# The order of every engine's queue, computed inside the kernel by list scheduling, for a two-layer retention and stick-breaking trunk

## The chip, the cores and the metric

The kernel runs on one core of one Trainium2 chip. The metric is device time in microseconds of one execution of the whole program. A core has five instruction queues that run side by side: TensorE (PE; its weight loads are listed apart as PEld), VectorE (DVE), ScalarE (ACT), GpSimd (POOL) and SyncE (SP), which here issues all the DMA transfers. Each queue is executed in its own order, which is fixed when the program is built. An instruction that waits for another engine or for a transfer holds back everything behind it in its queue.

## The reference

Two layers over a residual stream of 1024 tokens by 1024 features, in float32. Layer 0 is a retention with four heads, layer 1 a stick-breaking attention with eight heads whose keys and values come from one shared projection of the stream between the layers.

```python
u = rms_norm(h, ret_norm_pre[i])
q, k, v, g = jnp.split(u @ ret_w_in[i], ...)
q, k = rope(q, pos), rope(k, pos) * RET_QK_DIM ** -0.5
o = retention_chunkwise(q, k, v)              # o_t = sum_{s<=t} gamma_h^(t-s) (q_t . k_s) v_s
o = (o - mu) * lax.rsqrt(var + EPS)
y = (merge_heads(o) * jax.nn.silu(g)) @ ret_w_out[i]
h = h + rms_norm(y, ret_norm_post[i])
k_shared, v_shared = jnp.split(rms_norm(h, kv_norm) @ w_kv, [SB_QK_WIDTH], axis=-1)
...
q, g = jnp.split(rms_norm(h, sb_norm_pre[j]) @ sb_w_in[j], [SB_QK_WIDTH], axis=-1)
z = q @ k^T / sqrt(128)
weights = where(s < t, sigmoid(z_ts) * prod_{s<j<t} (1 - sigmoid(z_tj)), 0)
y = (merge_heads(weights @ v) * jax.nn.silu(g)) @ sb_w_out[j]
h = h + rms_norm(y, sb_norm_post[j])
```

## The kernel before

The stream is held transposed, features on the 128 partitions, and worked in two halves of 512 tokens. `run` (L1200) goes through four phases: retention for the first and the second half ("A", 0 and 1), then attention for the first and the second half ("C", 0 and 1). A phase has four turns, one for a retention head or for a pair of attention heads.

Every product is made of three float32r matmuls, `mm3` (L122 to L127): each operand is split into a rounded part and the rest, and high x high, high x low and low x high are summed in a PSUM bank. So nearly everything that enters a matmul passes first through `split` (L284 to L291): ACT writes the rounded part (L287, or L290 with a gain), then DVE writes the rest (L288, or L291). Weights come in 256 KB loads into the ring `wraw` of 6 buffers, in some phases also into `ko`, `S` and `vo` (`rings`, L1193), and are split into `whl`, which has 3 buffers of 1024 columns each.

Some projections are done with fewer products from sums and differences of blocks of weights and of activations: `vg` (L480) for retention, where DVE makes the weight sums (L507, L510, L513, L516), and `values` (L859) for attention, whose sums for later use are written to DRAM by `w_sums` (L799, sums L813 to L816).

Around the matmuls stand: the evacuation of banks (ACT copies L225, L531; DVE sums L227, L535, L946; gates L458, L459, L1001, L1002 and L1088); the rotary step `rope` (L425), which goes DVE, POOL (L431, L432), and then through a split; the norms, whose sums of squares are added on POOL (L256, L412, L730); the residual steps, in which loaded tiles are scaled and added on DVE or POOL (L720, L721, L1116, L1117); the transposes of gated outputs (L693) and of attention weights (L1064) on PE, followed by a split into `oT` or `AT`; and the stick-breaking product, `rows` (L1009): two sigmoids on ACT (L1027, L1028), two masks on POOL (L1032, L1033), a scan (L1034) and a product (L1035) on DVE. `finish` (L1122) does the last output projection, norm, and store.

PSUM has eight banks, two for each of the tags `ma`, `mb`, `z` and `o`. SBUF tiles have tags too; `BUFS` (L42) gives the buffers of each.

What sets the order: the program is written as lists of small steps that `merge` (L234) and `weave` (L147) interleave, so that side work (scores, gates, norms, the next weights through `ahead`, L157) is traced between the matmuls of a main projection. From the traced program the framework's own scheduler makes each engine's queue: it walks a simulated machine with its own table of times, and of the instructions that are ready there it issues the one that stands first in the program. It hands out a tag's buffers in that walk. The kernel sets no order edges of its own; the name `keep` (L80) is defined and never used.

## Time and profile before

| | |
|---|---|
| median of 3 runs | 1777.57 us (1775.73 to 1785.08) |
| the profiled execution, span from first to last instruction | 1776.7 us |
| mean granted TensorE clock | 0.993 |
| PE busy | 1717.6 us (97%), 8036 matmuls |
| PEld busy | 1417.6 us (80%) |
| DVE busy | 1295.9 us (73%), 2131 instructions |
| ACT busy | 871.0 us (49%), 1630 instructions |
| POOL busy | 282.9 us (16%), 377 instructions |
| DMA | 348.79 MB, 59.0% of 16 engines' span |

A group row of the profile names line, engine, operation, output tile <- input tiles and shape, then the count, busy time and mean time of one, and after the second bar the idle time of the engine just before these instructions, with what ended it. A timeline row has the start and the duration in us, and in brackets the engine's idle time before the instruction and what ended that. The view of waits lists who waited for whom: us in total, how often, the longest.

### The profile page before, as it was taken

What the parts mean: (1) busy time and instruction counts of PE and PEld (TensorE: products, weight loads), DVE (VectorE), ACT (ScalarE), POOL (GpSimd) and SP (SyncE); (2) the same over time, 40 slices, a digit from 0 to 9 for tenths busy, and PEclk for the clock granted to TensorE, in tenths of its full rate; (3) what the DMA queues carried; (4) which work ended last, traced back from release to release, by engine and by line L of the source; (5) the groups of instructions that cost most, each with busy time, mean ns of one, the idle gap of its engine ahead of it and who ended that gap; (6) DMA issues with size and microseconds to landing.
All of it is one profiled execution on the core that took longest, in us unless ns stands there. A gap on an engine that the chain in (4) does not pass through costs nothing.

```text
span 1776.7 us, 24193 instructions
## 1 busy us (share of the span) xinstructions
PE 1717.6 (97%) x8036; PEld 1417.6 (80%) x8036; DVE 1295.9 (73%) x2131; ACT 871.0 (49%) x1630; POOL 282.9 (16%) x377
## 2 busy tenths in 40 slices
PE   8999999999999899999999999999999999999997
PEld 7888788778788687878877888888887788888776
DVE  8757767898866968687788767668777656756765
ACT  6435545454444535355545435545564444545541
POOL 0210412332304320101112000000210010000003
PEclk9999999999999999999999999999999999999999
DMA  5226475658546756376886988568783763552513
GB/s 192 84 101 196 153 237 173 202 184 276 165 134 199 234 162 219 94 260 201 294 304 213 321 298 270 185 207 279 253 277 109 240 207 104 161 202 95 183 66 119
DMA packets 182380, 348.79 MB, mean 196 GB/s; under 512 B 20336, under 2 KB 24560, under 8 KB 182256
## 3 DMA queue, kind: packets, MB, share of 16 engines
q1 hardware_dynamic: 182256, 347.26, 59.0%
q8 instruction: 63, 1.03, 0.2%
q14 instruction: 61, 0.50, 0.1%
HBM read 273.78 MB, written 73.40 MB: 195 GB/s over the span
## 4 chain that ended last, share of the span: by engine, by line
issue 26%; PE 14%; DVE 10%; DMA 3%; POOL 2%; ACT 1%; SPq 0%; POOLq 0%; DVEq 0%; ACTq 0%
PE pmb L127 2%; PE pmb L125 2%; PE pmb L126 2%; PE pma L125 2%; PE pma L127 2%; PE pma L126 2%; DVE sgn L1034 2%; DVE whl L288 1%; DVE whl L291 1%; POOL sgn L1032 1%; DMA S<-y 1%; DVE A L1035 1%; PE po L126 1%; PE po L127 1%; PE po L125 1%
## 5 line engine op out<-in xcount | busy, mean ns | idle before, releaser
L288 DVE TENSOR_TENSOR whl<-wraw,whl 128x512 fp32r<-128x512 f32 x323 | 229.3, 737 | 50.3 <-ACT whl L287 50.0
L287 ACT ACTIVATE whl<-wraw 128x512 fp32r<-128x512 f32 x323 | 190.7, 624 | 100.0 <-PE pmb L127 42.9
L125 PE MATMUL pmb<-xh,whl 128*128 128x512 f32 x384 | 153.6, 400 | 1.6 <-DVE sg L1002 1.5
L125 PE MATMUL pma<-xh,whl 128*128 128x512 f32 x384 | 153.8, 400 | 0.0
L127 PE MATMUL pmb<-xh,whl 128*128 128x512 f32 x384 | 150.7, 393 | 0.0
L127 PE MATMUL pma<-xh,whl 128*128 128x512 f32 x384 | 150.7, 392 | 0.0
L126 PE MATMUL pma<-xh,whl 128*128 128x512 f32 x384 | 150.3, 391 | 0.0
L126 PE MATMUL pmb<-xh,whl 128*128 128x512 f32 x384 | 150.2, 391 | 0.0
L1032 POOL TENSOR_SCALAR_AFFINE_SELECT sgn<-sgn 128x128 f32<-128x128 f32 x64 | 28.3, 442 | 684.7 <-ACT sgn L1027 623.6
L1034 DVE TENSOR_TENSOR_SCAN sgn<-sgn 128x128 f32<-128x128 f32 (+3 forms) x64 | 89.0, 1390 | 26.8 <-POOL sgn L1032 26.8
L287 ACT ACTIVATE AT<-pz 128x512 fp32r<-128x512 f32 (+1 forms) x96 | 46.5, 486 | 119.7 <-PE pz L1064 119.7
L290 ACT ACTIVATE whl<-wraw,gn 128x256 fp32r<-128x256 f32 (+1 forms) x144 | 81.0, 602 | 48.4 <-PE pmb L127 30.5
L291 DVE SCALAR_TENSOR_TENSOR whl<-wraw,gn,whl 128x256 fp32r<-128x256 f32 (+1 forms) x144 | 83.4, 611 | 21.7 <-ACT whl L290 19.1
L125 PE MATMUL pmb<-oT,whl 128*128 128x512 f32 x240 | 95.7, 399 | 3.0 <-DVE sg L1002 3.0
L287 ACT ACTIVATE whl<-S 128x512 fp32r<-128x512 f32 x104 | 64.1, 629 | 66.8 <-DVE S L510 17.2
L127 PE MATMUL pmb<-oT,whl 128*128 128x512 f32 x240 | 94.6, 394 | 1.1 <-DVE whl L288 1.1
L126 PE MATMUL pmb<-oT,whl 128*128 128x512 f32 x240 | 94.1, 392 | 0.0
L288 DVE TENSOR_TENSOR AT<-pz,AT 128x512 fp32r<-128x512 f32 (+1 forms) x96 | 52.8, 552 | 54.0 <-ACT AT L287 53.8
L125 PEld LDWEIGHTS pmb<-xh,whl 128*128 128x128 f32 x384 | 72.5, 189 | 17.4 <-DVE sg L1002 3.7
L127 PEld LDWEIGHTS pmb<-xh,whl 128*128 128x128 f32 x384 | 72.4, 188 | 16.0
L127 PEld LDWEIGHTS pma<-xh,whl 128*128 128x128 f32 x384 | 72.4, 189 | 15.7
L126 PEld LDWEIGHTS pmb<-xh,whl 128*128 128x128 f32 x384 | 72.5, 189 | 13.5
(384 smaller groups left out, 4708.5 us busy)
## 6 DMA issues: line engine op xcount, KB each, us to landing
wraw<-in_wts_dram SPq DMA_DIRECT2D x522, 256.0 KB, 3.6
y<-f SPq DMA_DIRECT2D x120, 256.0 KB, 3.4
f<-y SPq DMA_DIRECT2D x88, 256.0 KB, 3.6
S<-in_wts_dram SPq DMA_DIRECT2D x44, 256.0 KB, 4.0
vo<-in_wts_dram SPq DMA_DIRECT2D x42, 256.0 KB, 4.7
ko<-in_wts_dram SPq DMA_DIRECT2D x40, 256.0 KB, 4.6
T<-AT SPq DMA_DIRECT2D x32, 256.0 KB, 3.6
sc<-T SPq DMA_DIRECT2D x16, 512.0 KB, 4.9
```

Source lines behind the costliest of these rows:

```text
L125: MM(p, lh, rh, start=start, stop=False, **kw)
L126: MM(p, lh, rl, start=False, stop=False, **kw)
L127: MM(p, ll, rh, start=False, stop=stop, **kw)
L287: A_.activation(dst[0], src, AF.Copy)
L288: V.tensor_tensor(dst[1], src, f32(dst[0]), ALU.subtract)
L290: A_.activation(dst[0], src, AF.Copy, scale=scale)
L291: V.scalar_tensor_tensor(dst[1], src, scale, f32(dst[0]), ALU.mult, ALU.subtract)
L1032: G.affine_select(n[:, dg], n[:, dg], [[-1, 128]], ALU.is_gt, 1.0, base=0, channel_multiplier=1)
L1034: V.tensor_tensor_scan(n[:, :W][:, ::-1], n[:, :W][:, ::-1], n[:, :W][:, ::-1], 1.0, ALU.mult, ALU.bypass)
L1035: V.tensor_tensor(a[:, :W - 1], a[:, :W - 1], n[:, 1:W], ALU.mult)
```

## The change

After the whole program is traced, `arrange` reads the instruction list of the block. For each instruction on the five engines it finds which tiles it reads and writes, at a grain of 32 elements, and from this the instructions that it must follow (`before`, and the mirror `after`); `behind` and `next` are the same for two reads on one engine. `_time` gives each a time that it holds its engine and a time until its result is there; `HAND` is the time of a hand-over to another engine.

`latest` counts latest starts backward: from the matmuls in the order of the program, through the read/write graph, and through the reuse of buffers (the last uses of a tile come before the first use of the tile that takes its buffer). `place` then runs the five engines forward in these times: when an engine is free, it takes of the instructions that are ready the one with the earliest latest start. A tag's tiles are opened in program order, each when one of the tag's buffers is free. DMA transfers share one ring; a two-input DVE operation that overlaps a long POOL addition is charged 400 ns more. Last, each engine's list is written out as order edges between neighbours, of a kind that fixes the order and needs no semaphore.

The diff, cut: `_size` and `_cells` (which count elements, and mark the touched 32-element cells of a tile) and some bookkeeping are left out.

```diff
+HAND = {"PE": 100.0, "DVE": 60.0, "Activation": 60.0, "Pool": 100.0, "SP": 50.0}
...
+def _time(s, chip):
+    n = _size(s.outs[0])
+    if s.eng == "PE":
+        full = str(s.ins[0].dtype) == "dt.float32" and not s.turns
+        t = max(216.0, n * 5 / 3 + 26.0) if full else max(110.0, n / 2.4 + 13.5)
+        return t, t + 165.0
+    bank = any(b.tensor.name in chip.banks for b in s.ins)
+    if s.eng == "DVE":
+        two = sum(_size(b) == n for b in s.ins) > 1
+        if s.op == "InstTensorTensor":
+            t = (n + 143) / 0.96
+        elif s.scan:
+            t = (2.08 * n + 150) / 0.96
+        elif s.op == "InstTensorScalarPtr" and two:
+            t = (n + 200) / 0.96
+        elif s.op == "InstBNStats":
+            t = (_size(s.ins[0]) + 152) / 0.96
+        else:
+            t = (n / 2 + 150) / 0.96
+        return max(t - 78.0, 60.0), t
+    if s.eng == "Activation":
+        t = (n + (200 if bank else 236)) / 1.2 + (95.0 if len(s.ins) > 1 else 0.0)
+        return t - 100.0, t
+    if s.eng == "Pool":
+        if s.op != "InstTensorTensor":
+            t = 250.0 + 0.62 * n
+        else:
+            t = 2.54 * n + 30.0 if n > 8 else 1280.0 if n == 4 else 720.0
+        return t, t
+    return n * 512 / 330.0, 4000.0
...
+def arrange(nc, tc, tag_of, bufs, banks):
...
+    order = place(steps, users, tags, tag_of, bufs, latest(steps, users, tags, bufs))
+    edge = mybir.DependencyInfo(mybir.DependencyClass.NoSync, mybir.DependencyReason.DATA)
+    for line in order.values():
+        for a, b in zip(line, line[1:]):
+            tc.add_manual_dep(steps[b].inst, steps[a].inst.name, edge, reason="order of the queue")
+
+def latest(steps, users, tags, bufs):
+    after = [set(s.after) for s in steps]
+    for tag, names in tags.items():
+        for a, z in zip(names, names[bufs[tag]:]):
+            f = users[z][0].k
+            for u in users[a]:
+                if u.k < f:
+                    after[u.k].add(f)
+    pe = [s for s in steps if s.eng == "PE"]
+    for a, z in zip(pe, pe[1:]):
+        after[a.k].add(z.k)
+    end = sum(s.busy for s in pe)
+    late = [0.0] * len(steps)
+    for s in reversed(steps):
+        t = end
+        for j in after[s.k]:
+            n = steps[j]
+            t = min(t, late[j] - (s.busy if s.eng == n.eng == "PE" else s.whole + (HAND[n.eng] if n.eng != s.eng else 20.0)))
+        late[s.k] = t if after[s.k] else end - s.whole
+    return late
+
+def place(steps, users, tags, tag_of, bufs, rank):
...
+        k = heapq.heappop(heaps[e])[1]
+        s = steps[k]
+        t = max(free[e], ready[k])
+        busy, whole = s.busy, s.whole
+        if e == "SP":
+            ring_free = max(t + 1000.0, ring_free) + busy
+            end, busy = ring_free + 1150.0, 400.0
+        else:
+            if e == "DVE" and s.op == "InstTensorTensor" and whole > 400.0 and not any(b.tensor.name in tag_of and tag_of[b.tensor.name] in ("ma", "mb", "z", "o") for b in s.ins):
+                if any(a < t + whole - 200.0 and z > t + 150.0 for a, z in pool_runs[-3:]):
+                    busy, whole = busy + 400.0, whole + 400.0
+            end = t + whole
+            if e == "Pool" and s.op == "InstTensorTensor" and whole > 600.0 and _size(s.outs[0]) > 100:
+                pool_runs.append((t, end))
+        free[e] = t + busy
+        order[e].append(k)
...
     def S(tag, shape, dt=F32):
         cnt[0] += 1
-        return sb.tile([128] + list(shape), dt, tag=tag, name=f"{tag}{cnt[0]}", bufs=BUFS[tag])
+        x = sb.tile([128] + list(shape), dt, tag=tag, name=f"{tag}{cnt[0]}", bufs=BUFS[tag])
+        tag_of[x[:].tensor.name] = tag
+        return x
...
     run()
+    arrange(nc, tc, tag_of, BUFS, banks)
```

More of the change, by code (lines that the diff above doesn't have):

```diff
@@ L1 @@
+import heapq
 import math
+from collections import defaultdict
 from contextlib import ExitStack
@@ L28, with _size, _cells @@
 G_PRE, G_POST, G_KV, G_SB, G_SBPOST = range(5)
+class Step:
+    pass
+HAND = {"PE": 100.0, "DVE": 60.0, "Activation": 60.0, "Pool": 100.0, "SP": 50.0}
+def _size(ap):
+    n = 1
+    for _, k in list(ap.ap)[1:]:
+        n *= k
+    return n
+def _cells(ap):
+    row = 1
+    for k in ap.tensor.shape[1:]:
+        row *= k
+    dims = sorted(((s, k) for s, k in list(ap.ap)[1:] if k > 1), key=lambda d: -abs(d[0]))
+    at, run = [ap.offset % row], 1
+    if dims and abs(dims[-1][0]) == 1:
+        s, run = dims.pop()
+        at = [at[0] - run + 1] if s < 0 else at
+    for s, k in dims:
+        at = [o + s * j for o in at for j in range(k)]
+    bits = 0
+    for o in at:
+        a, z = o // 32, (o + run - 1) // 32
+        bits |= ((1 << (z - a + 1)) - 1) << a
+    return bits
@@ new lines, in arrange @@
+def arrange(nc, tc, tag_of, bufs, banks):
+    chip = Step()
+    chip.banks = banks
+    steps, last, users = [], defaultdict(list), defaultdict(list)
+    for ins in nc.cur_bb.bb.instructions:
+        s = Step()
+        s.ins = [a.bass_ap for a in ins.ins if getattr(a, "bass_ap", None) is not None]
+        s.outs = [a.bass_ap for a in ins.outs if getattr(a, "bass_ap", None) is not None]
+        s.eng = str(ins.engine).split(".")[-1]
+        if not s.outs or s.eng not in HAND:
+            continue
+        s.inst, s.op, s.k = ins, type(ins).__name__, len(steps)
+        s.scan = bool(getattr(ins, "is_tensor_tensor_scan", False))
+        s.turns = bool(getattr(ins, "is_transpose", False))
+        s.before, s.after, s.behind, s.next = set(), set(), set(), set()
+        reads = [(b.tensor.name, _cells(b)) for b in s.ins if type(b.tensor).__name__ == "Tile"]
+        writes = [(b.tensor.name, _cells(b)) for b in s.outs if type(b.tensor).__name__ == "Tile"]
+        for name, m in reads:
+            s.before |= {o.k for o, n, w in last[name] if w and n & m}
+            s.behind |= set([o.k for o, n, w in last[name] if not w and n & m and o.eng == s.eng][-1:])
+        for name, m in writes:
+            s.before |= {o.k for o, n, w in last[name] if n & m}
+        for name, m in reads:
+            last[name].append((s, m, False))
+        for name, m in writes:
+            last[name] = [z for z in last[name] if z[1] & ~m] + [(s, m, True)]
+        s.tiles = sorted({name for name, _ in reads + writes})
+        for name in s.tiles:
+            users[name].append(s)
+        s.before.discard(s.k)
+        s.behind -= s.before | {s.k}
+        for p in s.before:
+            steps[p].after.add(s.k)
+        for p in s.behind:
+            steps[p].next.add(s.k)
+        s.busy, s.whole = _time(s, chip)
+        steps.append(s)
+    tags = defaultdict(list)
+    for name in sorted((n for n in users if n in tag_of), key=lambda n: users[n][0].k):
+        tags[tag_of[name]].append(name)
+    order = place(steps, users, tags, tag_of, bufs, latest(steps, users, tags, bufs))
[3 more added lines that the diff above has]
+            tc.add_manual_dep(steps[b].inst, steps[a].inst.name, edge, reason="order of the queue")
@@ new lines, in place, with met, give @@
+def place(steps, users, tags, tag_of, bufs, rank):
+    n = len(steps)
+    need = [len(s.before) + len(s.behind) for s in steps]
+    ready = [0.0] * n
+    opens = defaultdict(list)
+    for tag, names in tags.items():
+        for name in names:
+            opens[users[name][0].k].append(name)
+            for u in users[name]:
+                need[u.k] += 1
+    left = {name: len(u) for name, u in users.items()}
+    done_at = defaultdict(float)
+    slots = {tag: [0.0] * bufs[tag] for tag in tags}
+    turn, may = {tag: 0 for tag in tags}, {tag: 0.0 for tag in tags}
+    waits, heaps, free = ({e: [] for e in HAND} for _ in range(3))
+    free = {e: 0.0 for e in HAND}
+    order = {e: [] for e in HAND}
+    def met(k, t):
+        need[k] -= 1
+        ready[k] = max(ready[k], t)
+        if need[k] == 0:
+            heapq.heappush(waits[steps[k].eng], (ready[k], rank[k], k))
+    def give(tag):
+        if turn[tag] < len(tags[tag]) and slots[tag] and may[tag] is not None:
+            f = users[tags[tag][turn[tag]]][0]
+            turn[tag] += 1
+            t = heapq.heappop(slots[tag])
+            met(f.k, max(may[tag], t + HAND[f.eng] if t else 0.0))
+            may[tag] = None
+    for s in steps:
+        if need[s.k] == 0:
+            heapq.heappush(waits[s.eng], (0.0, rank[s.k], s.k))
+    for tag in tags:
+        give(tag)
+    ring_free, pool_runs = 0.0, []
+    for _ in range(n):
+        best = None
+        for e in HAND:
+            while waits[e] and waits[e][0][0] <= free[e]:
+                _, r, k = heapq.heappop(waits[e])
+                heapq.heappush(heaps[e], (r, k))
+            if heaps[e] or waits[e]:
+                t = free[e] if heaps[e] else waits[e][0][0]
+                if best is None or t < best[0]:
+                    best = (t, e)
+        t, e = best
+        while waits[e] and waits[e][0][0] <= t:
+            _, r, k = heapq.heappop(waits[e])
+            heapq.heappush(heaps[e], (r, k))
+        k = heapq.heappop(heaps[e])[1]
[14 more added lines that the diff above has]
+        order[e].append(k)
+        for name in opens[k]:
+            for u in users[name][1:]:
+                met(u.k, t)
+            may[tag_of[name]] = t
+            give(tag_of[name])
+        for j in s.next:
+            met(j, free[e])
+        for j in s.after:
+            met(j, free[e] if steps[j].eng == e == "PE" else end + (20.0 if steps[j].eng == e else HAND[steps[j].eng]))
+        for name in s.tiles:
+            left[name] -= 1
+            done_at[name] = max(done_at[name], end)
+            if left[name] == 0 and name in tag_of:
+                heapq.heappush(slots[tag_of[name]], done_at[name])
+                give(tag_of[name])
+    return order
@@ L43, in trunk @@
                 ko=2, sg=4, f2=6, acc=2, small=24, col=8, sc0=1, sc1=1, sc2=1, sc3=1, ma=2, mb=2, z=2, o=2)
-    cnt = [0]
+    cnt, tag_of, banks = [0], {}, set()
     def S(tag, shape, dt=F32):
         cnt[0] += 1
-        return sb.tile([128] + list(shape), dt, tag=tag, name=f"{tag}{cnt[0]}", bufs=BUFS[tag])
+        x = sb.tile([128] + list(shape), dt, tag=tag, name=f"{tag}{cnt[0]}", bufs=BUFS[tag])
+        tag_of[x[:].tensor.name] = tag
+        return x
     def PS(tag):
         cnt[0] += 1
-        return ps.tile([128, 512], F32, tag=tag, name=f"p{tag}{cnt[0]}", bufs=BUFS[tag])
+        x = ps.tile([128, 512], F32, tag=tag, name=f"p{tag}{cnt[0]}", bufs=BUFS[tag])
+        tag_of[x[:].tensor.name] = tag
+        banks.add(x[:].tensor.name)
+        return x
     def DRAM(name, dt):
```

## The prediction

> **What bounds the kernel now.** I read the page's shares first, then the busy time by stretch, then PE's waits, then the timeline around single stalls.

> ```profile
> span 1776.7 us, 24193 instructions
> ```
> ```profile
> 0.00:12.00 12.00, 6.13 (x16) 4.63 (x17) 6.65 (x14) 8.51 (x15) 0.20 (x4) 1.00 0.75 240
> 12.00:1740.00 1728.00, 1686.65 (x7825) 1389.05 (x7823) 1268.46 (x2066) 855.11 (x1600) 267.35 (x353) 1.00 0.60 198
> 1740.00:1777.00 37.00, 24.87 (x197) 23.95 (x197) 20.75 (x53) 7.34 (x18) 15.33 (x20) 0.89 0.34 118
> ```

> After the stretch come PE, PEld, DVE, ACT and POOL busy, the granted clock, the DMA share and GB/s. PE is busy for 1686.65 of the middle 1728.00 us; DVE, next, for 1268.46 (73%); DMA is at 0.60. PE is the bound. Idle on PE: 12.00 - 6.13 = 5.9 us at the start, 41.35 in the middle, 12.1 at the end. A new order can hardly touch the start (the first loads have to land) or the end (norm, scaling and store of the last columns), so the middle's 41.35 is what is at stake, with what hangs on it:

> ```profile
> 300.06 0.39 PE L126 MATMUL pma<-xh,whl 128*128 128x512 f32 x1
> 300.29 0.39 PE L127 MATMUL pma<-xh,whl 128*128 128x512 f32 x1
> ```

> A 512-column matmul shows 0.39 us, but the next starts 0.23 us after it. So PE is only "idle" once a start is 0.39 late, and each stall hides another 0.16 us. PE's waits (us in total, times, longest), the first and last of 24 rows with 46 waits:

> ```profile
> PE pma L125 <- ACT whl L287: 7.6, 3, 5.9
> PE pz L1064 <- DVE AT L288: 6.1, 3, 3.0
> PE pmb L125 <- DVE sg L1002: 4.5, 6, 2.7
> ...
> PE pmb L125 <- DVE f L430: 0.2, 1, 0.2
> ```

> The 5.9 is the start. Elsewhere nearly every row is released by DVE: a weight split, an operand split, a gate or bank evacuation. Yet DVE has a quarter of its time free, so the question is what it was doing when PE needed it. Four stalls show it.

> ```profile
> 953.66 0.58 ACT L287 ACTIVATE AT<-pz 128x512 fp32r<-128x512 f32 x1
> 954.24 0.96 DVE L720 SCALAR_TENSOR_TENSOR S<-S,gn,acc 128x512 f32<-128x512 f32 x1 [1.68 <-DMA S<-y]
> 955.73 0.69 DVE L721 TENSOR_TENSOR S<-S 128x512 f32<-128x512 f32 x1 [0.52 <-DMA S<-in_xT_dram]
> 956.34 0.68 DVE L288 TENSOR_TENSOR AT<-pz,AT 128x512 fp32r<-128x512 f32 x1
> 957.16 0.66 PE L1064 MATMUL pz<-ident,A 128*128 128x128 f32 x2 [3.02 <-DVE AT L288]
> ```

> ACT's half of the AT split ended at 954.24. DVE's half could have run then, but stood behind two residual steps (L720, L721), nothing PE needs soon, the second of them idle for a load. PE lost 3.02 us.

> ```profile
> 1390.47 0.37 ACT L287 ACTIVATE AT<-pz 128x256 fp32r<-128x256 f32 x1
> 1394.00 0.75 DVE L1116 SCALAR_TENSOR_TENSOR S<-S,gn,acc 128x512 f32<-128x512 f32 x1 [4.65 <-DMA S<-y]
> 1395.99 0.42 DVE L288 TENSOR_TENSOR AT<-pz,AT 128x256 fp32r<-128x256 f32 x1
> 1396.47 0.41 PE L126 MATMUL po<-AT,v 128*128 128x256 f32 x1 [2.31 <-DVE AT L288]
> ```

> The same: DVE sat 4.65 us at the head of its queue for a load of the output step, with the split that PE needed ready since 1390.84.

> ```profile
> 584.05 2.92 POOL L721 TENSOR_TENSOR vo<-vo,vo 128x512 f32<-128x512 f32 x1 [12.27 <-DVE S L510]
> 587.00 0.63 ACT L729 ACTIVATE vo<-vo 128x512 f32<-128x512 f32 x1 [2.31 <-POOL vo L721]
> 587.54 0.61 ACT L287 ACTIVATE whl<-S 128x512 fp32r<-128x512 f32 x1
> 588.20 0.50 PE L125 MATMUL pma<-whl,A 128*128 128x512 f32 x1 [0.88 <-ACT whl L287]
> ```

> ACT waited 2.31 us for a slow POOL sum, with a weight split behind it.

> ```profile
> 1710.95 2.01 DVE L1034 TENSOR_TENSOR_SCAN sgn<-sgn 128x896 f32<-128x896 f32 x1
> 1712.88 0.66 DVE L1002 TENSOR_TENSOR sg<-pmb,sg 128x512 f32<-128x512 f32 x1
> 1713.59 0.50 PE L125 MATMUL pmb<-oT,whl 128*128 128x512 f32 x1 [2.73 <-DVE sg L1002]
> ```

> A 2.01 us scan went ahead of the evacuation that frees PE's bank.

> A third loss follows the stalls: the granted clock.

> ```profile
> 750.00:764.00 14.00, 12.15 (x44) 8.73 (x43) 11.97 (x17) 5.40 (x10) 3.39 (x4) 0.88 0.59 180
> 950.00:964.00 14.00, 10.98 (x43) 8.70 (x42) 9.75 (x16) 4.42 (x9) 3.34 (x3) 0.76 0.78 248
> 1390.00:1404.00 14.00, 11.69 (x54) 9.68 (x53) 8.19 (x14) 4.57 (x10) 0.00 (x0) 0.88 0.71 230
> 1708.00:1722.00 14.00, 11.27 (x46) 8.60 (x45) 13.44 (x16) 6.69 (x14) 2.03 (x4) 0.88 0.05 19
> ```

> Around three of these stalls, and one near 755, the clock falls to 0.76 to 0.88 of full. Lost: 14 x (0.12 + 0.24 + 0.12 + 0.12) = 8.4 us of clock, of which PE worked 46.1 of 56 us: 6.9 us.

> **The change part by part.** The arithmetic, the tiles and the buffer counts stay; order edges add no semaphore and no instruction on an engine, so PE's own work stays. What changes is the order of all five queues, SP's loads included. Before, an instruction's rank is its place in the program and the times are the framework's. Now the rank is a latest start, counted back from the matmul order through buffer reuse, and the times are written out.

> *Removed.* Middle idle 41.35. Hidden part: about 42 middle waits x 0.16 = 6.7. Clock: 6.9. Together 55 us; with all of it gone the span is 1776.7 - 55 = 1722. All four stalls quoted are of a kind that a latest start repairs: AT's split, the weight split and the evacuation have early deadlines, residuals and scans late ones. Not all are: the L693 transposes alternate two pz banks with ACT and DVE, and a rope chain (DVE, POOL, ACT, DVE) is latency. As an estimate I take 80%: 44 us. The bounds are 60% (33), if the chains hold, and 95% (52).

> *The prices used.* The added table gives 512-column DVE sums (512 + 143)/0.96 = 682 ns and a 896-column scan (2.08 x 896 + 150)/0.96 = 2.10 us: the second is the 2.01 above, the first is the median here (min/median/max):

> ```profile
> L288 DVE TENSOR_TENSOR whl<-wraw,whl x323: 652/682/1782, 5.8 to 1704.6; 128x512 fp32r<-128x512 f32 x162
> ```

> A matmul of 512/2.4 + 13.5 = 227 ns is the spacing above. Two prices are low. A 256 KB load costs 1000 + 794 + 1150 ns = 2.94 us; the trace has more:

> ```profile
> wraw<-in_wts_dram SPq DMA_DIRECT2D x522, 256.0 KB, 3.6
> ko<-in_wts_dram SPq DMA_DIRECT2D x40, 256.0 KB, 4.6
> ```

> So DVE and ACT will be sent to some loads 0.7 to 1.7 us early and stand at the head of their queue, as at 1394.00, with a split behind them and PE behind that. Nothing in the trace prices this for the new order. DVE's own waits for weights are the nearest row:

> ```profile
> DVE S L507 <- DMA wraw<-in_wts_dram: 27.3, 20, 2.9
> ```

> Two of the 20 that PE felt:

> ```profile
> 571.69 0.69 DVE L507 TENSOR_TENSOR S<-wraw,wraw 128x512 f32<-128x512 f32 x1 [1.40 <-DMA wraw<-in_wts_dram]
> 573.03 0.50 PE L126 MATMUL po<-whl,xh 128*128 128x512 f32 x1 [1.10 <-DVE whl L288]
> 577.43 0.69 DVE L507 TENSOR_TENSOR S<-wraw,wraw 128x512 f32<-128x512 f32 x1 [1.68 <-DMA wraw<-in_wts_dram]
> 579.75 0.50 PE L126 MATMUL pmb<-whl,A 128*128 128x512 f32 x1 [0.98 <-DVE whl L288]
> ```

> They cost PE 1.10 + 0.98 + 2 x 0.16 = 2.4 us; taking these as all, one part in eleven of 27.3 came through, because weights are split ahead of PE. If twice or three times that much waiting for loads arises over the kernel (55 to 80 us), 5 to 7 us come through; doubled, since operand splits have less lead, 9 to 15. I take 9; the bounds are 3 and 17, and below nothing is excluded since an early head can only wait.

> The other low price is POOL beside DVE: a flat 0.4 us against a worst case of 1782 - 682 = 1.1. [...]

> On the clock, the rows show it halved after PE stalls of 2.3 to 3.0 us, so I count the 6.9 as gained once they shrink. [...]

> *Sum.* 44 - 9 = 35: the span falls to 1741.7. The median of the runs, 1777.57, is 0.9 above the profiled span, so **1742 us**; own range 1778 - (33 - 17) = 1762 to 1778 - (52 - 3) = 1729.

> **The rivals.** *Late heads win (slower).* The weight loads of the two DMA rows number 522 + 40 = 562, planned 0.7 to 1.7 us too short. A late one that reaches PE costs at least 0.7 + 0.16 us. Against the 44 removed, the break-even is 44/0.86 = 51 of them, one in eleven; at one in eight it is 70 x 0.86 = 60 us, 16 more than is removed: 1778 + 16 = 1794. SP adds to it: a load set ahead of its free buffer holds every load behind it. For: DVE already stood for loads at 954 and 1394. Against: weights are split ahead, so one part in eleven came through above, not all.

> [...]

> *Nothing moves.* The order before was also a list schedule; if PE's stalls are mostly latency of two-bank chains, stalls merely change place: 1769 to 1786, say 1777. Against it stand the four stalls, where the blocking work was plainly not urgent.

> *All of it.* Lead covers the late loads and the deadlines repair the chains too: 1722 to 1728.

> **How the numbers follow.** Forecast 0.50, all of it 0.13, POOL's lock 0.13, nothing moves 0.12, late heads 0.12. Half a per cent, 8.9 us, is about what a measurement of this kernel can tell from no change. The first three lie below 1768.7: faster 0.76; same 0.12; slower 0.12. Range 1720 to 1780: it leaves out late heads, 0.12, and some 0.05 of the ends.

> **What would show it.** PE's middle idle near 15 us instead of 41, PE's busy sum about unchanged; no row of PE's waits above 3 us but the start; clock about 1.0 at its four dips; residual steps and scans shifted to when PE has work. Late heads would show as DVE and ACT waits for DMA above the 27.3 row, with PE stalls behind them. [...] Middle idle at 35 or more makes the prediction wrong.

## The result and the profile after

The changed kernel takes 1733.9 us (median of 4 runs, 1733.82 to 1736.01) where the kernel before takes 1781.3 us beside it: ratio 0.9738, 95% interval 0.9711 to 0.9766. It is 2.6% faster, and the time lies in the range forecast (1742 us was the number). One reason given for it, the latest starts, and one term of its sum, the late loads, do not hold, as the experiments show.

Line numbers of the new kernel are 232 higher than those of before (L288 is L520 now). Its page begins:

```profile
span 1732.2 us, 24236 instructions
...
PE 1701.5 (98%) x8036; PEld 1415.4 (82%) x8036; DVE 1290.4 (74%) x2131; ACT 874.2 (50%) x1630; POOL 286.6 (17%) x377
```

By stretch, with the columns of before:

```profile
0.00:12.00 12.00, 6.26 (x18) 4.53 (x19) 5.71 (x11) 7.63 (x13) 0.20 (x4) 1.00 0.75 252
12.00:1696.00 1684.00, 1671.75 (x7837) 1388.44 (x7836) 1265.05 (x2071) 859.91 (x1602) 271.36 (x353) 1.00 0.60 203
1696.00:1733.00 37.00, 23.50 (x185) 22.46 (x183) 19.64 (x51) 6.68 (x16) 15.09 (x20) 0.82 0.30 105
```

PE's idle time in the middle is 1684.00 - 1671.75 = 12.25 us, where it was 41.35. The span is 44.5 us shorter: 29.1 from that idle time, 16.1 from PE's busy sum (1717.6 to 1701.5), less 0.7 at the two ends. The busy sum could fall although the matmuls are the same 8036, because a matmul's row grows when it runs at half clock or waits a little: a 512-column row is 0.39 us at full clock, 0.63 us in the half-clock stretch at 740, and 0.50 us in several rows behind a wait. PE worked at half clock for 16.2 us of the middle before and for 3.4 after, which makes 12.8 / 2 = 6.4 us. Waits in the middle fell from 42 to 11, which makes 31 x 0.16 = 5.0. The other 4.7 us lie mostly in starts that were less than 0.15 us late: between neighbouring 512-column matmuls of the middle at full clock, what start-to-start distances have above 0.227 us without being a wait sums to 27.1 us before and 23.8 after.

Of PE's 13 rows of waits (L1296 is the transpose, L1064 before), the first four, the split of AT and the last:

```profile
PE pma L357 <- ACT oT L522: 5.7, 1, 5.7
PE pz L357 <- ACT qk L519: 2.6, 1, 2.6
PE pz L1395 <- DVE acc L1389: 2.2, 1, 2.2
PE pmb L357 <- DVE sg L1234: 1.9, 2, 1.3
...
PE pz L1296 <- DVE AT L520: 0.7, 1, 0.7
...
PE pma L357 <- DMA sc<-T: 0.2, 1, 0.2
```

The first is the start, the third belongs to the end. AT's splits cost PE 0.7 us (6.1 before), the gates 1.9 (4.5). What DVE and ACT stood for, after:

```profile
DVE S L739 <- DMA wraw<-in_wts_dram: 13.9, 13, 2.8
...
DVE S L1348 <- DMA S<-y: 2.1, 2, 1.7
ACT sgn L894 <- POOL small L882: 29.8, 17, 3.6
```

and, of before, the two of these rows that the prediction doesn't show:

```profile
DVE S L1116 <- DMA S<-y: 8.3, 3, 4.7
ACT sgn L662 <- POOL small L650: 90.0, 30, 6.3
```

Summed over all tiles, DVE's waits for DMA fell from 71.0 us (47) to 41.7 (35), and ACT's waits for POOL from 162.9 to 64.8. The step for which DVE stood 4.65 us at 1394, L1116, waits 1.7 us at most now, as L1348.

The scan ahead of a gate is still there in the last turn:

```profile
1666.72 2.01 DVE L1266 TENSOR_TENSOR_SCAN sgn<-sgn 128x896 f32<-128x896 f32 x1
1668.65 0.66 DVE L1234 TENSOR_TENSOR sg<-pmb,sg 128x512 f32<-128x512 f32 x1
1669.37 0.50 PE L357 MATMUL pmb<-oT,whl 128*128 128x512 f32 x1 [1.32 <-DVE sg L1234]
```

It costs 1.32 us now, where it cost 2.73. The largest stall that is left in the middle is a rotary chain:

```profile
738.20 0.50 PE L357 MATMUL pz<-qk 128*128 128x512 f32 x1 [2.56 <-ACT qk L519]
738.53 0.40 PE L358 MATMUL pz<-qk 128*128 128x512 f32 x1
740.36 0.78 PE L359 MATMUL pz<-qk 128*128 128x512 f32 x1 [1.44 <-DVE qk L520]
740.94 0.63 PE L357 MATMUL pz<-qk 128*128 128x512 f32 x1
```

The rows of 0.78 and 0.63 us are matmuls at half clock (granted 0.50 from 740.41 to 743.82). In the kernel before, PE lost 1.8 us to this chain (0.74, 0.84 and 0.24 us at 755 to 758); here it is 2.56 + 1.44 = 4.0.

### The profile page after: what moved, and what is told of

Same layout as the page of the kernel before. It is cut to its first block, busy times and chain, and to the rows that moved or that the text cites. A ratio compares the mean times of both kernels' runs of the same rounds, so it can differ in the third digit from the quotient of the medians.

```text
span 1732.2 us, 24236 instructions
## 1 busy us (share of the span) xinstructions
PE 1701.5 (98%) x8036; PEld 1415.4 (82%) x8036; DVE 1290.4 (74%) x2131; ACT 874.2 (50%) x1630; POOL 286.6 (17%) x377
## 5 line engine op out<-in xcount | busy, mean ns | idle before, releaser
L520 DVE TENSOR_TENSOR whl<-wraw,whl 128x512 fp32r<-128x512 f32 x323 | 229.9, 739 | 71.8 <-ACT whl L519 69.7
L1266 DVE TENSOR_TENSOR_SCAN sgn<-sgn 128x384 f32<-128x384 f32 (+4 forms) x64 | 88.5, 1386 | 25.3 <-POOL sgn L1264 24.9
L522 ACT ACTIVATE whl<-wraw,gn 128x256 fp32r<-128x256 f32 (+1 forms) x144 | 80.7, 602 | 49.6 <-PE pmb L359 36.2
L520 DVE TENSOR_TENSOR AT<-pz,AT 128x512 fp32r<-128x512 f32 (+1 forms) x96 | 52.9, 554 | 61.7 <-ACT AT L519 61.5
## 6 DMA issues: line engine op xcount, KB each, us to landing
wraw<-in_wts_dram SPq DMA_DIRECT2D x522, 256.0 KB, 3.5
y<-f SPq DMA_DIRECT2D x120, 256.0 KB, 3.6
f<-y SPq DMA_DIRECT2D x88, 256.0 KB, 3.9
S<-in_wts_dram SPq DMA_DIRECT2D x44, 256.0 KB, 4.3
vo<-in_wts_dram SPq DMA_DIRECT2D x42, 256.0 KB, 5.0
ko<-in_wts_dram SPq DMA_DIRECT2D x40, 256.0 KB, 4.5
T<-AT SPq DMA_DIRECT2D x32, 256.0 KB, 5.7
```

Source lines behind the costliest of these rows:

```text
L520: V.tensor_tensor(dst[1], src, f32(dst[0]), ALU.subtract)
L522: A_.activation(dst[0], src, AF.Copy, scale=scale)
L1266: V.tensor_tensor_scan(n[:, :W][:, ::-1], n[:, :W][:, ::-1], n[:, :W][:, ::-1], 1.0, ALU.mult, ALU.bypass)
```

## The experiments

All kernels are the changed one with one edit ("short prices" and the last two with several). Ratios are to the kernel before, run beside them (1780 to 1782 us).

| kernel | us | ratio, 95% interval |
|---|---|---|
| the change | 1733.9 | 0.9738 [0.9711, 0.9766] |
| edges on DVE and ACT only | 1754.8 | 0.9853 [0.9834, 0.9873] |
| edges on DVE, ACT and SP only | 1743.3 | 0.9789 [0.9772, 0.9806] |
| edges on PE, POOL and SP only | 1799.7 | 1.0108 [1.0088, 1.0128] |
| rank = place in the program | 1732.3 | 0.9723 [0.9708, 0.9738] |
| loads 0.8 us longer | 1738.8 | 0.9762 [0.9746, 0.9779] |
| short prices | 1746.5 | 0.9802 [0.9779, 0.9824] |
| short price, POOL | 1747.0 | 0.9803 [0.9781, 0.9824] |
| short price, scan | 1747.7 | 0.9810 [0.9784, 0.9836] |
| short price, matmul | 1737.5 | 0.9750 [0.9724, 0.9776] |
| no charge beside POOL | 1743.2 | 0.9795 [0.9778, 0.9812] |
| old rank and short prices | 1739.2 | 0.9770 [0.9756, 0.9785] |
| the same, chosen early | 1770.4 | 0.9944 [0.9927, 0.9960] |

Four of the twelve times expected came in: the short scan price, the short matmul price, no charge beside POOL, and choosing early. With the old rank the time is 0.7 us below the nearer range. The other seven lie outside every range that was named.

**Which queue carries it.** My theory was that DVE's and ACT's order is what counts; the rival was the order of the loads.

```diff
-    for line in order.values():
+    for line in [order[e] for e in ("DVE", "Activation")]:
```

> Order edges on VectorE and ScalarE alone; the other three queues stay with the framework's scheduler. If the gain (before 1777.6, after 1733.9) is the order on these two engines, nearly all of it stays: 1733 to 1748 us, middle idle of TensorE 12 to 25 us. If the gain is TensorE's own order or the order of the loads, 1762 to 1782 us.

> Order edges on TensorE, GpSimd and SyncE alone; VectorE and ScalarE stay with the framework. If the gain is the order on VectorE and ScalarE: 1765 to 1785 us, with residual steps and scans again ahead of splits. If it is TensorE's own order or that of the loads: 1733 to 1748 us.

> Edges on VectorE, ScalarE and SyncE only; TensorE's and GpSimd's queues are left to the framework, whose order there is nearly the change's anyway. With edges on VectorE and ScalarE alone 1754.8 us was measured, 21 us above the whole change. If those 21 us belong to the order of the loads (theory), this kernel comes to 1733 to 1738 us, VectorE's waits for DMA fall from 61 back to about 42 us, and TensorE's middle idle to 12 to 14 us. If they belong to the small differences in TensorE's or GpSimd's queue (rival), it stays at 1750 to 1756 us.

With DVE and ACT alone 26.9 us of the 47.4 are there; with PE, POOL and SP alone nothing is gained and 18 us are lost. With SP added to DVE and ACT 37 us are there, so the loads' order is worth some 11 us (by the ratios, 0.9853 and 0.9789) on top of the order of DVE and ACT. That it needs this order, because SP's queue serves a schedule that isn't run otherwise, is argued: no kernel has SP's edges alone. DVE's waits for DMA fit it, 61.1 us without SP's edges, 36.2 with them, 80.3 in the kernel with PE, POOL and SP. The last 9 us hang on the edges of PE and POOL, and so on small differences: without them POOL's order is all but the same, and 250 of PE's 8036 matmuls stand three places or more from where the change has them.

**The rank.** The prediction said that the latest starts repair the stalls. The rank of before, an instruction's place in the program, goes back in, and all else stays.

```diff
-    order = place(steps, users, tags, tag_of, bufs, latest(steps, users, tags, bufs))
+    order = place(steps, users, tags, tag_of, bufs, [float(s.k) for s in steps])
```

> All edges and all prices as in the change, but the rank of an instruction is its place in the program instead of its latest start. If the deadlines make the gain: 1762 to 1785 us, since the four kinds of inversion come back. If the written-out times make it (an engine no longer stands for a load or a GpSimd sum that the plan took for early), 1733 to 1748 us. In between would be a share for each.

It takes 1732.3 us; the two intervals overlap. Its middle:

```profile
12.00:1692.40 1680.40, 1670.31 (x7824) 1385.35 (x7823) 1261.54 (x2066) 859.47 (x1601) 281.75 (x353) 1.00 0.60 203
```

The idle time is 10.1 us, without any deadline. The latest starts are worth nothing here. My reason falls.

The change's largest stall even goes with them. PE waits at least 2.2 us for the rotary chain near 740 in the change and in each kernel of the table whose DVE edges come from the latest starts. With the place in the program as rank, PE waits 0.77 us there, and for another product:

```profile
739.64 0.47 PE L511 MATMUL pz<-sgn,onesr 128*128 128x512 f32 x1 [0.77 <-DVE sgn L504]
```

The clock granted over this middle is 1.00 (over the whole execution 0.997, in the change 0.996). The deadlines are not the only way to that stall: choosing early, below, has it under the old rank too (2.68 us). Why the deadlines put the rotary products late was not looked into.

**The loads' price.** The prediction took 9 us for loads planned too short.

```diff
-            end, busy = ring_free + 1150.0, 400.0
+            end, busy = ring_free + 1950.0, 400.0
```

> A load is priced 0.8 us longer (3.74 us for 256 KB, close to the 3.6 us of the trace); all else as in the change. If late loads at the head of a queue still cost the 9 us of my sum: 1723 to 1729 us, and VectorE's waits for loads fall. If weights are split so far ahead that nothing comes through: 1731 to 1737 us, no change.

```profile
DVE S L739 <- DMA wraw<-in_wts_dram: 7.8, 7, 3.4
```

The waits for weights fall, 13.9 to 7.8 us (all of DVE's for DMA 41.7 to 19.6), as the truer price should make them; but all of DVE's waits for DMA come to only 22 to 25 us in the three kernels with a shorter load price too, so the fall alone proves little. The time does not fall (1738.8, intervals overlap). What is longer is one stall, in a chain that has no load in it (ACT waits for a product of DVE there):

```profile
882.38 0.77 PE L493 MATMUL pz<-ones,acc 128*128 128x1 f32 x3 [3.04 <-ACT A L1260]
```

Half clock follows it, in which PE works 6.35 us. Without the stall the time would be some 3.04 + 0.16 + 6.35 / 2 = 6.4 us less, as an estimate: 1732.4, which is 1.5 us below the change and not 9. So the late loads cost PE next to nothing that a price can give back.

**The other prices.** If not the rank, then the prices? The short prices are a matmul at 213 ns, a 896-column scan at 1.09 us, POOL's one-column operations at 150 and 464 ns, its additions at 2.34 ns an element and its other operations by 128 + 0.91 n, a load 0.19 us shorter, and nothing charged beside POOL.

```diff
-            t = (2.08 * n + 150) / 0.96
+            t = (n + 150) / 0.96
...
-            t = 2.54 * n + 30.0 if n > 8 else 1280.0 if n == 4 else 720.0
+            t = 2.34 * n + 30.0 if n > 8 else 958.0 if n == 4 else 464.0 if "mhalf" in s.ins[1].tensor.name else 150.0
```

> The change's own scheduler, buffer rule and edges, but with the prices close to those of the framework's table: a 512-column matmul 213 ns for 227, scans at half, sums of one column on GpSimd 150 ns and powers 464 or 958 ns for 720 or 1280, loads 0.2 us shorter, no charge for VectorE beside GpSimd. After the run with the program's place as rank, the deadlines are out as the cause. If the written-out times make the gain: 1762 to 1785 us. If it is the scheduler itself (one walk over five queues, buffers opened in program order): 1730 to 1742 us.

> Only GpSimd's prices short (one-column sums 150 ns and powers 464 or 958 ns in place of 720 and 1280). If ScalarE's waits for GpSimd at the head of its queue (163 us in the kernel before, 65 in the changed one) carry the gain: 1750 to 1770 us and those waits above 120 us. If they are a side show: 1731 to 1740 us.

> Only the scan's price short: 1.09 us for 2.10 us at 896 columns. If scans planned too short push splits late in the attention phases: 1742 to 1760 us, the whole loss after 880 us. If not: 1731 to 1738 us.

> Only the matmul's price short: 213 ns for 227 at 512 columns, 53 for 110 at 128, so that the plan lets TensorE run 6% faster than it does and the other queues are ordered for a machine in which they are later than in truth. If the plan has to keep step with TensorE: 1745 to 1770 us. If not: 1731 to 1740 us.

All short prices together cost 12.6 us, POOL's alone 13, the scan's alone 14, the matmul's nothing that can be told (the interval overlaps the change's). They don't add up. For the scan and for POOL the timeline has a stall that the wrong price explains. With the short scan:

```profile
1678.87 2.01 DVE L1266 TENSOR_TENSOR_SCAN sgn<-sgn 128x896 f32<-128x896 f32 x1
1680.80 0.66 DVE L1234 TENSOR_TENSOR sg<-pmb,sg 128x512 f32<-128x512 f32 x1
1681.52 0.55 PE L357 MATMUL pmb<-oT,whl 128*128 128x512 f32 x1 [2.73 <-DVE sg L1234]
```

This is the stall of 2.73 us of the kernel before, back: the scan is taken for half its length and goes ahead. With POOL's short prices:

```profile
381.26 0.55 POOL L880 TENSOR_TENSOR small<-small,cc 128x1 f32<-128x1 f32 x1 [4.10 <-DVE small L876]
381.88 0.94 POOL L881 TENSOR_TENSOR small<-small,mhalf 128x1 f32<-128x1 f32 x1
382.90 0.77 POOL L882 TENSOR_TENSOR small<-small,small 128x1 f32<-128x1 f32 x1
383.70 0.78 ACT L894 ACTIVATE sgn<-po,small,small 128x512 f32<-128x512 f32 x1 [3.13 <-POOL small L882]
384.53 0.50 PE L357 MATMUL po<-v,sc 128*128 128x512 f32 x1 [2.12 <-ACT sgn L894]
```

Three tiny operations are planned at 0.15 + 0.46 + 0.15 us and take 0.55 + 0.94 + 0.77. ACT is sent to their result early and stands 3.13 us, and PE 2.12 behind it. Over the kernel that wait is

```profile
ACT sgn L894 <- POOL small L882: 79.8, 25, 6.9
```

against 29.8 with the prices of the change, and 90.0 before.

Neither stall is the whole of its 13 or 14 us, and not all of the rest is shown to be the price. With the short scan PE is idle for 19.4 us of the middle (12.25 in the change) and works 12.8 us at half clock (3.4); one of its new stalls, 1.82 us at 938.46, stands behind a weight split that took 1.77 us beside a POOL addition, with no scan in it. And the ACT step that stalls at 882 with the longer load price stalls PE for 3.09 us with the short matmul price and for 3.70 with all short prices. So a part of what such an edit costs is where the new order happens to leave a stall.

**The charge beside POOL.** The 400 ns for a two-input DVE operation beside a long POOL addition are set to 0. The expectation speaks of a lock between the two. Of that the trace of before shows times: DVE's 512-column weight splits take at most 694 ns with no POOL operation beside them and up to 1782 ns with one.

> The charge of 400 ns for a two-input VectorE operation beside a long GpSimd addition is set to 0; all else as changed. If the lock between the two is a cost that the order has to plan for (rival of the prediction), stalls behind such pairs come back: up to 13 us more (1747 us), as with the other prices taken away. If the 0.4 us is too small to move an order (theory: few such pairs stand ahead of something that TensorE waits for soon), 1732 to 1737 us.

It costs 9 us (1743.2; the intervals don't overlap). That is more than I expected of so few pairs. One of its stalls stands behind a POOL addition that took long:

```profile
571.62 5.91 POOL L962 TENSOR_TENSOR acc<-acc,vo 128x512 f32<-128x512 f32 x1 [1.42 <-ACT vo L961]
579.26 0.63 ACT L961 ACTIVATE vo<-vo 128x512 f32<-128x512 f32 x1 [5.22 <-POOL vo L953]
580.95 0.49 PE L357 MATMUL pma<-whl,A 128*128 128x512 f32 x1 [1.37 <-ACT whl L519]
```

The median of this addition is 1.29 us in the changed kernel. Here it takes 5.91 us; then ACT stands 5.22 us for the next POOL sum, with a weight split behind it. This stall is 1.4 of the 9 us. The other large one near it (2.36 us at 572.88) has no POOL operation in its chain. So the charge pays here; how much of the 9 us comes from long operations like this one is open, and whether 400 ns is too little was not tried.

**What is left: the walk.** With old rank and old prices something of the gain should be gone, if rank and prices are all of the change. Prices as short as before and the rank of before stand in for the framework's choice.

> Rank by place in the program and all the short prices together, in the change's own walk: the two things that the change says it replaces, both put back. Each alone left the gain nearly whole (1732.3 us with the old rank, 1746.5 us with the short prices). If the two add up, 1744 to 1748 us, and some 33 us of the gain lie in neither but in the walk itself (how loads and buffers are handed out in it). If a latest start makes up for short prices, so that only both together bring the loss back (rival), 1765 to 1781 us.

> As the run with both the old rank and the short prices, and besides, VectorE, ScalarE and GpSimd choose an instruction as soon as the fourth before it has begun, so that the choice is made among what is ready by then, as a queue that is filled ahead would make it. If the framework's loss comes from choosing early (theory), it rises from about 1746 towards 1770 to 1781 us, with TensorE's waits for VectorE from about 20 towards 40 us. If not (rival), it stays at 1742 to 1752 us.

The edit of the second, beside the two above (`began` holds the planned starts on each engine):

```diff
+    def open_at(e):
+        q = 4 if e in ("DVE", "Activation", "Pool") else 0
+        return (began[e][-q] if len(began[e]) >= q else 0.0) if q else free[e]
...
-            while waits[e] and waits[e][0][0] <= free[e]:
+            while waits[e] and waits[e][0][0] <= open_at(e):
...
-                t = free[e] if heaps[e] else waits[e][0][0]
+                t = open_at(e) if heaps[e] else waits[e][0][0]
```

With both put back the time is 1739.2 us, 41 us below the kernel before. So neither rank nor price is the core. When besides the engines choose four instructions ahead, among what is ready by then, the time is 1770.4: 31 of those 41 us are gone. Its middle (this kernel's lines are 7 higher again):

```profile
12.00:1731.60 1719.60, 1687.63 (x7820) 1394.81 (x7818) 1273.17 (x2066) 858.00 (x1600) 272.52 (x353) 0.99 0.59 199
```

PE is idle for 32.0 us here; in the kernel that doesn't choose early it is 16.1 us over the same part. And half clock stands for 34.1 us of the middle, where that kernel has none; PE works 30.3 us of it, which costs 15 us. Together that is the 31. PE's first four rows of waits (the first row holds the 5.9 us of the start):

```profile
PE pma L364 <- ACT whl L526: 8.6, 2, 5.9
PE pmb L364 <- DVE sg L1241: 6.4, 4, 3.1
PE pz L366 <- DVE qk L527: 3.4, 2, 1.9
PE po L364 <- ACT sgn L901: 3.1, 2, 1.9
```

The second row is the gate behind a scan once more (3.1 us at 1706.83). Choosing early on DVE, ACT and POOL is shown to cost 31 us in this walk. That the framework loses its time in the same way is argued, not shown, and three things speak against it: this kernel's order on DVE is no nearer to that of before than the order without early choice is; 10 us remain between them; and PE's waits differ in kind. In the kernel before, PE waits 40.7 us for DVE and 9.6 for ACT (the start's 5.9 among them, here too). Choosing early raises its waits for DVE only from 17.3 to 21.9 us, where I had expected about 40, and those for ACT from 8.6 to 18.5.

## Why the prediction was right, and where it wasn't

- **The bound** held: the time fell with PE's middle idle and what hangs on it. DVE's busy time is 1290.4 us, and PE's idle time fell to 12.25, a little below the 15 named.
- **The removed time** was forecast at 44 of 55 us. Counted the same way it is 29.1 idle + 5.0 hidden + 6.4 clock = 40.5. With the 4.7 us of small delays that I had not counted, less the 0.7 at the ends, it is 44.5. The size was right, but by luck in part: no row stood under the 80%, and the delays make up what the counted parts fell short. One sign that I named contradicts my own sum: PE's busy time was to stay "about unchanged", while the hidden part and the clock, 6.7 + 6.9 us, lie in it. It fell by 16.1.
- **The 9 us for loads sent too early** were not there. It is this term that makes the forecast 8 us too long. DVE's waits for weights were to double or triple from 27.3 us and fell to 13.9; PE waited 0.2 us for a transfer; and a longer price, which cut the waits once more, gained nothing. The row I scaled from (two PE stalls of about 1 us behind such waits) was true; that such waits should double or triple over the kernel was not. As I read it, a head sent too early costs only where nothing was split ahead.
- **"All four stalls are of a kind that a latest start repairs"** is the step that failed. They are mostly repaired, and so they are with the rank of before (1732.3 us), so the latest start is not what repairs them. The rotary chain, which I had named as one that it would not repair, even got longer with it: 4.0 us where it was 1.8, and with the old rank PE has no wait for it. In this walk a choice at the time the engine is free, among what is ready then by the plan, was enough. As I read it, an AT split that is ready when DVE comes free goes before a residual whose load isn't there, whatever either's deadline.
- **Prices** I had treated as a risk alone (two are low). They are a part of the gain: the scan's and POOL's each cost 13 to 14 us when one alone is short, the charge beside POOL 9 when it is left out, and all together 12.6; with the old rank the short prices cost 7 (1732.3 to 1739.2).
- **The clock** dips in one place of the middle, at 740 (0.50 for 3.41 us), behind the rotary chain (the dip near 755 before). The other three dips went with their stalls, as forecast; this one stayed.
- **Late heads, nothing moves, all of it** did not come: DVE's waits for DMA fell, the middle idle is far under 35, and the span is 10 us above the 1722 of "all of it".

**POOL's lock** has a chance of 0.13 in the prediction. No run shows that operations of DVE and POOL exclude each other; what the runs show are times. DVE's busy time is 1295.9 us before and 1290.4 after. In the trace of before, the 254 weight splits on DVE with no POOL operation beside them take at most 694 ns; of the 69 that overlap one, the longest takes 1782. POOL's operations are long at times too, as this row of the new kernel shows (min/median/max):

```profile
L882 POOL TENSOR_TENSOR small<-small,small x32: 185/190/2887, 85.9 to 802.9; 128x1 f32<-128x1 f32 x32
```

A one-column operation takes 190 ns in the median and up to 2.9 us here. The one of 2.9 us, at 792.36, lies beside four DVE operations with two inputs, one behind the other, the longest 1.23 us. The change's price of 720 ns is well above the median; with POOL's prices short, ACT's wait for this row is 79.8 us, with the change's 29.8.

What stays open is why the framework's own walk is 41 us worse than this one with its rank and short prices. Early choice is a candidate by its size, 31 us, and its waits are of another kind. That this walk opens a tag's tiles in program order, and that it plans the loads on one ring, are rivals that were not tried.

## What to carry to other kernels

When the bound engine's stalls stand behind work that was not urgent, look first at when the choice is made and by which times: an order chosen at the moment the engine is free, with measured prices for the slow operations, took out 29 of 41 us of idle time here; choosing four instructions ahead gave 31 us of the time back in this walk; and a cleverer priority added nothing. Set the edges on all the queues that were planned together, the loads' queue with them. A price is worth mending where an engine would be sent early to a result that stands in front of the bound engine; loads with lead were no such place here. Before a few us between two such orders are put down to an edit, look whether they are one stall that has moved.

## What the runs showed of the hardware

```profile
1669.80:1673.20 3.40, 1.80 (x10) 1.15 (x8) 3.40 (x3) 1.38 (x3) 0.21 (x1) 1.00 0.75 231
1673.20:1676.60 3.40, 2.68 (x14) 2.25 (x15) 3.40 (x6) 1.20 (x2) 0.00 (x0) 1.00 0.59 179
1393.30:1396.70 3.40, 1.09 (x7) 0.69 (x6) 2.67 (x5) 0.00 (x0) 0.00 (x0) 1.00 0.63 234
1396.70:1400.10 3.40, 3.40 (x12) 2.82 (x12) 2.29 (x5) 0.60 (x1) 0.00 (x0) 0.50 0.83 245
```

Stalls of 2.33 us (at 1673.92) and 2.31 (at 1396.47): the first is spread over two stretches, 1.60 and 0.72 us, and the clock stays; the second lies in one, 2.31, and the next runs at 0.50. So in these two the idle time within one such stretch tells them apart, and the length of the stall does not. Counted in these steps, between 12 and 1700 us of the profiles before and after, the three full-clock stretches with the most idle time on PE were followed by half clock: 2.64 us (at 736.99, after), 2.31 (at 1393.28, before) and 2.21 (at 952.95, before). Of the 15 with 1.18 to 1.80 us idle one was, with 1.44 us at 754.98 before, where the longest single wait is 0.84 us; of those with less, none.

A stretch at half clock costs up to 1.7 us, as an estimate, half of its 3.41. Behind the stall of 2.31 us at 1396.47 one such stretch followed, behind the one of 3.02 us at 957.16 two, behind the one of 2.33 us at 1673.92 none. Choosing early lost in both ways: 16 us of idle time and 15 of clock.
